# A two-block transformer on one Trainium2 core: the opening stage issued in one written order, with half of the first gate computed on TensorE

## The chip, the core and the metric

The kernel runs on one core of a Trainium2 chip. The core has five engines with a queue each: TensorE for matmuls (PE; its weight loads are shown as PEld), VectorE (DVE), ScalarE (ACT), GpSimd (POOL) and SyncE, whose queue (SP) issues nearly all loads from the chip's memory. Each engine works through its own queue in order; semaphores tie the queues together. The metric is the device time of one execution in microseconds, lower is better. Of the kernel before there are three timed runs, with a median of 959.78 us (957.72 to 960.89), and one profiled execution.

## The reference, cut to what matters

Two blocks run one after the other on a sequence of 256 tokens of width 1024. The first block is two layers deep: a causal pooling layer and an attention layer, each followed by an MLP with a squared ReLU (1024 to 4096 to 1024), and all of them modulated by rows that are computed from a condition vector `c`. The second block mixes a gated delta rule with a forgetting attention and ends in a SwiGLU. Nothing of the change lies behind the first MLP's first chunks, so this is the part that counts (layer 0):

```python
c_act = jax.nn.silu(c)
mod = c_act @ w_mod[0] + b_mod[0]                      # 1024 x 6144, read once
sh1, sc1, g1, sh2, sc2, g2 = jnp.split(mod, 6, axis=-1)
h = modulate(rmsnorm(x, norm_mix[0]), sh1, sc1)        # h * (1 + sc1) + sh1
y = pool_mixer(h, w_pool[0], pool_scale[0])            # trailing means, 4 groups of 256 channels
x = x + g1[:, None, :] * y
h = modulate(rmsnorm(x, norm_mlp[0]), sh2, sc2)
x = x + g2[:, None, :] * squared_relu_mlp(h, w_up[0], w_down[0])
...
def pool_mixer(h, w_pool, pool_scale):                 # per group g: (window mean - token) @ w_pool[g]
    ...
    return y * pool_scale
def squared_relu_mlp(h, w_up, w_down):
    a = jax.nn.relu(h @ w_up)
    return (a * a) @ w_down
```

All tensors are float32. Products of full precision are made of three matmuls on split operands: a high part (`_h`, `_hi`), which ACT rounds, and a low part (`_l`, `_lo`), the rest, which DVE subtracts.

## The kernel before, in words

The 256 tokens are two tiles of 128. Weights arrive in loads of 512 KB or 1 MB (128 partitions of 4 or 8 KB) and are split in pieces of 128x1024 by one ACT and one DVE instruction each (`piece_hi`, L275, and `piece_lo`, L281).

Everything from the first load to the first two of the eight chunks of the first MLP's up projection is one stage, in which all five queues follow the order in which the program issues (`manual_schedule`). The steps of this stage, with the names that the order lists and the prediction use:

- The rows `c` and the columns of biases and norms (`vecs`), `x` and the pooling bands are loaded. `crow` is silu(c) on all partitions, `c32` silu(c) as columns. The norm factors of `x` (`n0`) are worked out and `x` is multiplied by them (L759).
- Sections: a half (512 columns) of one of the six modulation parts comes as two loads of 1 MB (`wms`, SP L680), is multiplied by `c32` on PE (`sec`, L722: 4 matmuls of 32x512 for each load, which the trace counts as 8), copied by ACT (`secr`, L727), turned into a column of four blocks on PE (`secc`, L734) and finished by DVE (L741, L744). Before, the mixer's scale and shift and the MLP's scale are made in this way.
- Columns: the mixer's gate and the MLP's shift are made on DVE, by one multiply-and-sum of 128x1024 for each of the eight blocks of 128 channels (`wmp`, L807, and `wms`, L459), from loads of 512 KB per block.
- Pooling: window sums on PE (`pk`, L751 to L753), scale on ACT (L771), shift on DVE (L775), split (L779, L782), the products with `w_pool` (`pool`, L292 to L294), the gate on ACT (`pool_o`, L813), transposes to token rows (`xadd`, L820) and the additions to `x` (L526).
- The MLP's norm: sums of squares on ACT (L358), factors (L686, L341 to L352), the normalized tokens (`mlp_xn`, L839 on DVE and L841 on ACT), transposes to feature columns (`mlp_tp`, L848), scale and shift on ACT (`mlp_hf`, L856), split.
- The up projection of chunks 0 and 1: for each of eight blocks of channels and each of the two chunks 6 matmuls of 128x512 (`up<-wu_...,mlp_...`), 96 in all; the weights are `wu00` and `wu01`, two loads of 1 MB each, split in four pieces. Two loads of chunk 2 (`wu02`) close the stage.

Loads go into three pools of buffers: `mraw` (two of 1 MB), `raw` (three of 1 MB) and the pieces (five pairs `whi`, `wlo` of 512 KB each). SP waits for a buffer at the issue of its load, and what stands behind in its queue waits too. The loads' own semaphores let eight loads be under way.

The order of this stage is made by `Plan`: each step has an engine, a cost in us and its needs; the planner walks through time and takes what can start first, the longest remaining way first. Loads keep the order in which they are written down. Three lines show the kind:

```python
plan = Plan({"dma": 3.0, "vec": 11.0, "act": 9.5, "pe": 6.0})
op(f"win{g}", "pe", 2.6, [], windows, g)
op(n, "vec", 1.4, [f"g1{kt // 2}"], lambda kt=kt: gate_sum(kt, loaded[f"g1{kt // 2}"][kt % 2]))
```

Behind the stage the chunks follow one another (`up` of 128x256 for the next chunk, `dn` for the down projection), in an order that the scheduler sets.

Of the kernel before, what the change touches and what calls it, by code (L numbers as in the profile page):

```python
# [14 lines left out]
P = 128  # L15
# [124 lines left out]
class Plan:  # L140

    LAG = {"dma": 1.1}

    def __init__(self, free):
        self.free, self.ops = dict(free), {}

    def op(self, name, eng, cost, needs, f, *args):
        self.ops[name] = [eng, cost, list(needs), f, args]  # L150

    def run(self):
        ops = self.ops
        way = {}
        after = {n: [] for n in ops}
        for n, o in ops.items():
            for k in o[2]:
                after[k].append(n)

        def to_end(n):  # L160
            if n not in way:
                way[n] = ops[n][1] + max([to_end(k) for k in after[n]], default=0.0)
            return way[n]

        loads = [n for n, o in ops.items() if o[0] == "dma"]
        done, order, left = {}, [], dict(ops)
        while left:
            ready = []
            for n, (eng, cost, needs, _, _) in left.items():
                if eng == "dma" and n != loads[0] or any(k not in done for k in needs):  # L170
                    continue
                t = max([self.free[eng]] + [done[k] for k in needs])
                ready.append((t, -to_end(n), n))
            first = min(ready)
            eng, cost = ops[first[2]][:2]
            t, _, n = min((r for r in ready if ops[r[2]][0] == eng and r[0] <= first[0] + 0.02), key=lambda r: r[1])
            if eng == "dma":
                loads.pop(0)
            self.free[eng] = t + cost
            done[n] = t + cost + self.LAG.get(eng, 0.1)  # L180
            order.append((t, n))
            del left[n]
        self.done = done
        for t, n in order:
            ops[n][3](*ops[n][4])


def build(tc, a, out):
# [4 lines left out]
    with ctx:  # L193
# [139 lines left out]

        def rsqrt_col(v, n, name, rows=P, scale=1.0):

            y = work.tile([P, n], F32, tag=f"rs_y{n}", name=f"{name}_y", bufs=4)
            h = work.tile([P, n], F32, tag=f"rs_h{n}", name=f"{name}_h", bufs=2)
            t = work.tile([P, n], F32, tag=f"rs_t{n}", name=f"{name}_t", bufs=2)
            y, h, t = y[:rows], h[:rows], t[:rows]
            if n <= 2:  # L340
                pool.tensor_tensor(y, v, halves_of[:rows, :n], ALU.pow)  # L341
            else:
                vec.tensor_scalar(y.bitcast(I32), v.bitcast(I32), -0.5, RSQRT_MAGIC, ALU.mult, ALU.add)
            steps = 1 if n <= 2 else 3
            vec.tensor_scalar(h, v, -0.5 * (scale if steps == 1 else 1.0), None, ALU.mult)
            for i in range(steps):
                if n == 1:
                    vec.scalar_tensor_tensor(t, y, y, h, ALU.mult, ALU.mult)
                else:
                    vec.tensor_tensor(t, y, y, ALU.mult)  # L350
                    vec.tensor_tensor(t, t, h, ALU.mult)
                vec.scalar_tensor_tensor(y, t, 1.5 * (scale if steps == 1 else 1.0), y, ALU.add, ALU.mult)  # L352
            assert steps == 1 or scale == 1.0
            return y
# [347 lines left out]
        ones1 = [t2k(f"ones1{hf}") for hf in range(2)]
        for hf in range(2):
            ps = acc_tile(f"ones1p{hf}")
            pe.matmul(ps, ones[:1], rows0[:1, D + hf * 512:D + (hf + 1) * 512], start=True, stop=True)
            act.activation(ones1[hf], ps, AF.Copy)

        def section_load(sec, hf, q, where):  # L710
            src = a["w_mods"][sec, hf, q]
            return first_load(where, (src[:, :1024], src[:, 1024:]), f"wms{sec}{hf}{q}")

        sums32 = {}

        def section_product(sec, hf, q, rr):
            if q == 0:
                sums32[sec, hf] = acc_tile(f"sec{sec}{hf}")
            ps = sums32[sec, hf]
            for k in range(4):  # L720
                rows = slice(32 * k, 32 * k + 32)
                pe.matmul(ps[rows], c32[:, 4 * q + k], rr[k // 2][:, k % 2 * 512:(k % 2 + 1) * 512], start=q == 0,  # L722
                          stop=q == 1)

        def section_rows(sec, hf):
            t = t2k(f"secr{sec}{hf}")
            act.activation(t, sums32[sec, hf], AF.Copy)  # L727
            sums32[sec, hf] = t

        def section_turn(sec, hf):  # L730
            t = sums32[sec, hf]
            ps = sums32[sec, hf] = acc_tile(f"secc{sec}{hf}")
            for k in range(4):
                pe.matmul(ps[:, k:k + 1], t[:, k * P:(k + 1) * P], ones[:, 0:1], start=True, stop=True)  # L734

        def section_columns(sec, hf):
            s = (1, 0, 4)[sec]
# [16 lines left out]

        ss = [sums_of(x[:, t], f"n0{t}") for t in range(2)]
        y = pair_rstd(ss, "n0")
        xn0 = [big_tile(f"n0{t}")[:, :D] for t in range(2)]
        for t in range(2):
            vec.tensor_scalar(xn0[t], x[:, t], y[:, t:t + 1], None, ALU.mult)  # L759
        pks = [(mm_tile, tp_tile)[g % 2](f"pk{g}").rearrange("p (k n) -> p k n", k=2) for g in range(4)]  # L760
        def windows(g):
# [1366 lines left out]
```

## Time and profile before

| what | value |
|---|---|
| median of three timed runs | 959.78 us (957.72 to 960.89) |
| the profiled execution's own time | 960.81 us |
| its span, first to last instruction | 959.0 us |
| mean granted clock of TensorE | 0.98 |
| PE, PEld busy | 914.6 us (95%), 799.3 us (83%) |
| DVE, ACT busy | 642.4 us (67%), 497.7 us (52%) |
| loaded over the span | 198.31 MB, mean 207 GB/s |

The profiled execution takes 1.81 us more than its span and 1.03 us more than the median of the timed runs. All times below are us from the start of the span. In the 40 slices of the page (24 us each) PE is busy for 6, 7 and 6 tenths of the first three and for 9 from then on, but for two slices of 8 and the last of 6. The 96 matmuls of the first two up chunks begin at 68.53 and the next chunk's at 93.61: between these times and the start lies the stage that is changed.

### The profile page before, as it was taken

How to read it: one execution, taken by the hardware profiler on the slowest of the kernel's cores; microseconds unless marked ns; L12 is line 12 of the kernel's file. 1: busy time of each engine (PE TensorE's matmuls, PEld its weight loads, DVE VectorE, ACT ScalarE, POOL GpSimd, SP SyncE). 2: the span in 40 equal slices, each digit the busy share in tenths (PEclk: the TensorE clock that was granted, in tenths of full speed). 3: DMA queues.
4: the chain of work that ended last, by engine and by line, in shares of the span. 5: the costliest groups of instructions: out<-in, count | busy, mean ns of one | idle time of the engine just before them, and what ended most of it. 6: DMA issues, size and time to landing. Idle time of an engine off the chain costs nothing.

```text
span 959.0 us, 15265 instructions
## 1 busy us (share of the span) xinstructions
PE 914.6 (95%) x6021; PEld 799.3 (83%) x6021; DVE 642.4 (67%) x1230; ACT 497.7 (52%) x881; POOL 12.5 (1%) x22
## 2 busy tenths in 40 slices
PE   6769999999998999999999998999999999999996
PEld 3548889988797987889999967899988799999995
DVE  1587789789698674885556567698557765454544
ACT  2465535445466674644455535676455564444442
POOL 0000000000000000000000002000000000000000
PEclk9779999999999999999999999899999999999998
DMA  9979879889466460785565644233022555555531
GB/s 349 419 314 352 286 291 405 338 287 376 147 234 250 157 228 33 266 284 181 192 222 176 211 144 151 78 120 129 11 79 89 198 175 177 181 187 203 176 132 45
DMA packets 34555, 198.31 MB, mean 207 GB/s; under 512 B 4186, under 2 KB 6818, under 8 KB 14002
## 3 DMA queue, kind: packets, MB, share of 16 engines
q1 hardware_dynamic: 34484, 197.34, 57.8%
q8 instruction: 47, 0.77, 0.3%
q14 instruction: 24, 0.20, 0.1%
HBM read 196.24 MB, written 1.09 MB: 206 GB/s over the span
## 4 chain that ended last, share of the span: by engine, by line
PE 84%; DVE 5%; DMA 4%; issue 2%; ACT 2%; POOL 0%; SPq 0%; DVEq 0%; POOLq 0%; ACTq 0%
PE up L292 6%; PE up L293 6%; PE up L294 6%; PE dn L292 6%; PE dn L293 6%; PE dn L294 6%; PE gu L294 4%; PE gu L293 4%; PE gu L292 4%; PE qk L321 3%; PE fd L293 2%; PE fd L292 2%; PE fd L294 2%; DMA wms<-in_w_mods_dram 2%; PE cp L292 1%
## 5 line engine op out<-in xcount | busy, mean ns | idle before, releaser
L292 PE MATMUL up<-mlp_hi,wu_h 128*128 128x256 f32 x416 | 118.4, 285 | 0.0
L293 PE MATMUL up<-mlp_lo,wu_h 128*128 128x256 f32 x416 | 118.0, 284 | 0.0
L294 PE MATMUL up<-mlp_hi,wu_l 128*128 128x256 f32 x416 | 117.8, 283 | 0.0
L275 ACT ACTIVATE wd_h<-wd_r 128x1024 fp32r<-128x1024 f32 x58 | 61.4, 1059 | 74.1 <-PE up L293 44.1
L281 DVE TENSOR_TENSOR wd_l<-wd_r,wd_h 128x1024 fp32r<-128x1024 f32 x58 | 70.8, 1223 | 40.2 <-ACT wd_h L275 40.0
L275 ACT ACTIVATE wu_h<-wu_r 128x1024 fp32r<-128x1024 f32 x58 | 60.9, 1062 | 61.9 <-PE dn L294 47.0
L292 PE MATMUL dn<-wd_h,a 128*128 128x512 f32 x232 | 91.8, 396 | 0.0
L293 PE MATMUL dn<-wd_l,a 128*128 128x512 f32 x232 | 90.8, 392 | 0.0
L292 PE MATMUL gu<-f_hi,wgu_h 128*128 128x256 f32 x320 | 90.7, 283 | 0.0
L294 PE MATMUL gu<-f_hi,wgu_l 128*128 128x256 f32 x320 | 90.6, 283 | 0.0
L293 PE MATMUL gu<-f_lo,wgu_h 128*128 128x256 f32 x320 | 90.6, 283 | 0.0
L294 PE MATMUL dn<-wd_h,a 128*128 128x512 f32 x232 | 90.3, 389 | 0.0
L281 DVE TENSOR_TENSOR wu_l<-wu_r,wu_h 128x1024 fp32r<-128x1024 f32 x58 | 70.3, 1223 | 27.0 <-ACT wu_h L275 26.9
L281 DVE TENSOR_TENSOR wgu_l<-wgu_r,wgu_h 128x1024 fp32r<-128x1024 f32 x44 | 53.6, 1225 | 51.2 <-ACT wgu_h L275 51.2
L292 PEld LDWEIGHTS up<-mlp_hi,wu_h 128*128 128x128 f32 x416 | 79.7, 192 | 1.0 <-issue 0.5
L293 PEld LDWEIGHTS up<-mlp_lo,wu_h 128*128 128x128 f32 x416 | 79.7, 192 | 1.0 <-issue 0.5
L294 PEld LDWEIGHTS up<-mlp_hi,wu_l 128*128 128x128 f32 x416 | 79.8, 192 | 0.0
L275 ACT ACTIVATE wgu_h<-wgu_r 128x1024 fp32r<-128x1024 f32 x44 | 46.6, 1062 | 61.9 <-PE gu L293 29.4
L293 PEld LDWEIGHTS gu<-f_lo,wgu_h 128*128 128x128 f32 x320 | 61.4, 192 | 0.3
L292 PEld LDWEIGHTS gu<-f_hi,wgu_h 128*128 128x128 f32 x320 | 61.4, 192 | 0.4
L294 PEld LDWEIGHTS gu<-f_hi,wgu_l 128*128 128x128 f32 x320 | 61.4, 192 | 0.0
L292 PEld LDWEIGHTS dn<-wd_h,a 128*128 128x128 f32 x232 | 43.6, 188 | 10.0 <-issue 1.4
(770 smaller groups left out, 2286.3 us busy)
## 6 DMA issues: line engine op xcount, KB each, us to landing
wu_r<-in_w_up_dram SPq DMA_DIRECT2D x32, 1024.0 KB, 5.1
wd_r<-in_w_down_dram SPq DMA_DIRECT2D x32, 1024.0 KB, 5.3
wgu_r<-in_w_gu_dram SPq DMA_DIRECT2D x22, 1024.0 KB, 5.2
wmc<-in_w_modc_dram SPq DMA_DIRECT2D x16, 1024.0 KB, 7.1
wmg<-in_w_modg_dram SPq DMA_DIRECT2D x12, 1024.0 KB, 6.7
wfd_r<-in_w_fd_dram SPq DMA_DIRECT2D x11, 1024.0 KB, 4.9
wi_r<-in_w_in_dram SPq DMA_DIRECT2D x10, 1024.0 KB, 5.3
wqk_r<-in_w_qk_dram SPq DMA_DIRECT2D x8, 1024.0 KB, 5.8
```

Of the source, the lines that this page charges most:

```text
L275: act.activation(hi, r, AF.Copy)
L281: vec.tensor_tensor(lo, r, hi.bitcast(F32), ALU.subtract)
L292: pe.matmul(ps, l[0], r[0], start=first, stop=False)
L293: pe.matmul(ps, l[0], r[1], start=False, stop=False)
L294: pe.matmul(ps, l[1], r[0], start=False, stop=last)
L321: f(*a, **k)
```

## The change

`Plan` and its costs go; the steps are registered by name, and a written list, `FIRST_STEPS`, calls them in its order. A word of the list can carry the buffer pool of a load (`raw`, `mraw`, `split`) or the bank pool of a PE result (`acc`, `mm`, `tp`), which were fixed by rule before. Besides:

- `rows` (c) and `vecs` are loaded through ACT's queue; SP's first load is `x`.
- The squares of `x` are issued ahead of silu(c) on ACT, and the norm factors multiply the pooling bands (128x576 and 128x512 on DVE) where they multiplied `x` (two of 128x1024).
- The gate's second half (channel blocks 4 to 7) is made as a section (`s21`): two loads, two PE products, a copy, a turn and two small DVE operations, where it was four DVE sums. The first half stays on DVE. The loads have the same bytes.
- A section's turned column goes into the bank of its sums.
- One of the four sums of squares of the MLP's norm (tile 1, second half) is made on DVE. The norm factors are two steps (`y1`, `y2`), and another step can stand between them.

```diff
-class Plan:
-    ...
+FIRST_STEPS = """
+s101:mraw s001:mraw bn win2:acc s100:raw s000:raw wp:raw wph1 g2:split s00m0:acc ident s110:split s00m1
...
+        sq00 tok6 wu00 tok7 s30m0:acc add01 s30m1 add11 sq11 sq10 sq01 y1 col0 y2 s30r xn0v s30t ...
...
-        sp.dma_start(rows0[:1, :2 * D], a["c"])
+        act.dma_start(rows0[:1, :2 * D], a["c"])
...
-        sp.dma_start(vecs, a["vecs"])
+        act.dma_start(vecs, a["vecs"])
...
+        ss = [sums_of(x[:, t], f"n0{t}") for t in range(2)]
+        y0 = rsqrt_col(pair_sums(ss, "n0"), 2, "n0", scale=32.0)
         for hf, c in enumerate(halves):
             act.activation(crow[:, c], crp[hf], AF.Silu)
...
+        SECTIONS = (1, 0, 2, 4)
+        HALVES = ((0, 0), (0, 1), (1, 0), (1, 1), (2, 1), (3, 0), (3, 1))
...
         def section_turn(sec, hf):
-            t = sums32[sec, hf]
-            ps = sums32[sec, hf] = acc_tile(f"secc{sec}{hf}")
             for k in range(4):
-                pe.matmul(ps[:, k:k + 1], t[:, k * P:(k + 1) * P], ones[:, 0:1], start=True, stop=True)
+                pe.matmul(sums32[sec, hf][:, k:k + 1], secr[sec, hf][:, k * P:(k + 1) * P], ones[:, 0:1], start=True,
+                          stop=True)
...
+            if s == 2:
+                vec.tensor_tensor(gate[:, h4], col, vcol(V_BG)[:, h4], ALU.add)
+                vec.tensor_tensor(gate[:, h4], gate[:, h4], vcol(V_POOL)[:, h4], ALU.mult)
+                return
...
-        for t in range(2):
-            vec.tensor_scalar(xn0[t], x[:, t], y[:, t:t + 1], None, ALU.mult)
...
+        def bands_normed():
+            vec.tensor_scalar(bands[:, B_FIRST:], bands[:, B_FIRST:], y0[:, 0:1], None, ALU.mult)
+            vec.tensor_scalar(bands[:, :B_FIRST], bands[:, :B_FIRST], y0[:, 1:2], None, ALU.mult)
...
+            sq = t2k("poolsq")
+            vec.tensor_tensor_reduce(out=sq, in0=xs, in1=xs, scale=1.0, scalar=0.0, op0=ALU.mult, op1=ALU.add,
+                                     accum_out=ss[t][:, hf:hf + 1])
...
-        def norm_factors():
-            ys.append(pair_rstd(ss, "mlp0n"))
+        def norm_factors(first):
+            if first:
+                ys.append(pair_sums(ss, "mlp0n"))
+                ys.append(rsqrt_guess(ys[0], 2, "mlp0n", scale=32.0))
+            else:
+                ys[0] = rsqrt_step(*ys[1], 2, 32.0)
...
-        plan.run()
+        for word in FIRST_STEPS.split():
+            name, *where = word.split(":")
+            f, args = steps.pop(name)
+            f(*args, *where)
...
-    d["w_mods"] = f(wm[0, [1, 0, 4]])
+    d["w_mods"] = f(np.concatenate([wm[0, 1], wm[0, 0], wm[0, 2, 1:], wm[0, 4]]))
...
-    d["w_modp"] = f(wc[0, [2, 3]])
+    d["w_modp"] = f(np.concatenate([wc[0, 2, :4], wc[0, 3]]))
```

Names in the order below: `wmsAB...` are loads of section A (before: 0 scale, 1 shift, 2 MLP scale; now 2 is the gate and 3 the MLP scale), half B; `wmp0`, `wmp1` (before `wmp` and `wms0` to `wms6`) loads of the gate's and the MLP shift's columns.

SP's queue around the loads of the up weights, before:

```order
L680 DMA wms211_432<-in_w_mods_dram 128x1024 x2
L220 DMA wu00_r0_450<-in_w_up00_dram 128x2048
L220 DMA wu01_r0_462<-in_w_up00_dram 128x2048
L680 DMA wms0_480<-in_w_modp_dram 128x1024 x2
L680 DMA wms2_506<-in_w_modp_dram 128x1024 x2
L220 DMA wu00_r2048_526<-in_w_up00_dram 128x2048
L220 DMA wu01_r2048_572<-in_w_up00_dram 128x2048
L680 DMA wms4_594<-in_w_modp_dram 128x1024 x2
L680 DMA wms6_622<-in_w_modp_dram 128x1024 x2
```

and now:

```order
L190 DMA wu01_r0_307<-in_w_up00_dram 128x2048
L698 DMA wms300hi_315<-in_w_mods_dram 128x1024
L698 DMA wms300lo_316<-in_w_mods_dram 128x1024
L698 DMA wms301hi_387<-in_w_mods_dram 128x1024
L698 DMA wms301lo_388<-in_w_mods_dram 128x1024
L738 DMA wmp10_440<-in_w_modp_dram 128x1024 x2
L698 DMA wms310_463<-in_w_mods_dram 128x1024 x2
L190 DMA wu00_r0_471<-in_w_up00_dram 128x2048
L698 DMA wms311hi_512<-in_w_mods_dram 128x1024
L698 DMA wms311lo_513<-in_w_mods_dram 128x1024
L738 DMA wmp12_549<-in_w_modp_dram 128x1024 x2
L738 DMA wmp14hi_592<-in_w_modp_dram 128x1024
```

Before, all four loads of `wu00` and `wu01` and both of the MLP scale's second half stood ahead of the last four shift columns, with `wu01_r2048` waiting for a `raw` buffer in the midst. Now `wu01_r0` stands ahead of the MLP scale, and the loads alternate between sections, columns and up weights.

DVE's queue from the additions to `x` on, before:

```order
L526 TENSOR_TENSOR x_81<-xadd00_411,x_81 128x512
L526 TENSOR_TENSOR x_81<-xadd10_412,x_81 128x512
L281 TENSOR_TENSOR wu00_l0_488<-wu00_r0_450,wu00_h0_487 128x1024
L526 TENSOR_TENSOR x_81<-xadd01_483,x_81 128x512
L526 TENSOR_TENSOR x_81<-xadd11_484,x_81 128x512
L459 ISA wms0_480,modcol0_102<-wms0_480,crow_96,vecs_84 128x1024
L459 ISA modcol0_102 128x1
L741 TENSOR_TENSOR modcol0_102<-secc20_490,vecs_84 128x4
L744 SCALAR_TENSOR_TENSOR modcol0_102<-modcol0_102,vecs_84 128x4
L686 TENSOR_SCALAR mlp0n_v_530<-pool0_ss_154 128x1
L686 TENSOR_SCALAR mlp0n_v_530<-pool1_ss_155 128x1
L345 TENSOR_SCALAR mlp0n_h_534<-mlp0n_v_530 128x2
```

and now:

```order
L251 TENSOR_TENSOR wu01_p0_423<-wu01_r0_307,wu01_p0_423 128x1024
L507 TENSOR_TENSOR x_81<-xadd00_395,x_81 128x512
L507 TENSOR_TENSOR x_81<-xadd10_396,x_81 128x512
L507 TENSOR_TENSOR x_81<-xadd01_452,x_81 128x512
L507 TENSOR_TENSOR x_81<-xadd11_453,x_81 128x512
L828 ISA poolsq_486,pool1_ss_147<-x_81 128x512
L828 ISA pool1_ss_147 128x1
L663 TENSOR_SCALAR mlp0n_v_492<-pool0_ss_146 128x1
L663 TENSOR_SCALAR mlp0n_v_492<-pool1_ss_147 128x1
L310 TENSOR_SCALAR mlp0n_h_496<-mlp0n_v_492 128x2
L440 ISA wmp10_440,modcol0_102<-wmp10_440,crow_96,vecs_84 128x1024
L440 ISA modcol0_102 128x1
```

Before, a weight piece (`wu00_l0`) stood between the two pairs of additions, and a column sum with two small operations between them and the norm's sums. Now the four additions and a sum of squares follow each other, and the column sum stands inside the norm factors, behind `mlp0n_h`.

PE's queue from the transposes of the normalized tokens to the first up matmuls, before:

```order
L848 MATMUL mlp0_tp2_575<-ident_85,mlp0_xn0_542 128x128
L848 MATMUL mlp0_tp2_575<-ident_85,mlp0_xn1_544 128x128
L292 MATMUL up000_584<-wu00_h0_487,mlp0_hi_156 128x512
L293 MATMUL up000_584<-wu00_l0_488,mlp0_hi_156 128x512
L294 MATMUL up000_584<-wu00_h0_487,mlp0_lo_157 128x512
L292 MATMUL up001_588<-wu00_h0_487,mlp0_hi_156 128x512
L293 MATMUL up001_588<-wu00_l0_488,mlp0_hi_156 128x512
L294 MATMUL up001_588<-wu00_h0_487,mlp0_lo_157 128x512
```

and now:

```order
L854 MATMUL mlp0_tp1_528<-ident_85,mlp0_xn0_506 128x128
L854 MATMUL mlp0_tp1_528<-ident_85,mlp0_xn1_518 128x128
L706 MATMUL sec31_538<-wms310_463,c32_98 32x512 x4
L262 MATMUL up010_553<-wu01_p0_423,mlp0_hi_148 128x512
L263 MATMUL up010_553<-wu01_p0_423,mlp0_hi_148 128x512
L264 MATMUL up010_553<-wu01_p0_423,mlp0_lo_149 128x512
L262 MATMUL up011_557<-wu01_p0_423,mlp0_hi_148 128x512
L263 MATMUL up011_557<-wu01_p0_423,mlp0_hi_148 128x512
L264 MATMUL up011_557<-wu01_p0_423,mlp0_lo_149 128x512
```

Before, six blocks were transposed and the sections were all done when the up matmuls began, with chunk 0 ahead. Now the first product of the MLP scale's second half stands between four transposed blocks and the up matmuls, with chunk 1 ahead.

## Rows read from the trace of the kernel before

**Rows 1.** The page, the span in 40 slices: DMA engines' busy share, tenths

```profile
DMA  9979879889466460785565644233022555555531
```

**Rows 2.** Busy time of each engine, granted clock, DMA share, GB/s by 5 us

```profile
40.00:45.00 5.00, 4.00 (x17) 3.71 (x18) 4.96 (x17) 4.75 (x14) 0.00 (x0) 0.50 1.03 422
...
60.00:65.00 5.00, 0.84 (x5) 0.79 (x5) 3.92 (x13) 3.88 (x8) 0.70 (x1) 0.50 0.71 297
65.00:70.00 5.00, 4.30 (x16) 3.46 (x17) 5.00 (x9) 4.50 (x8) 0.00 (x0) 0.50 0.28 61
```

**Rows 3.** The chain that ended last: start, length, what (0 to 140 us)

```profile
21.21 11.68 DMA wpool<-in_w_pool_dram
...
68.17 0.31 ACT mlp_hi L779
...
68.53 0.80 PE up L292
```

**Rows 4.** What SP's queue waited for, total, times, longest (0 to 110 us)

```profile
SPq L220 <- DVE wu_l L281: 28.6, 4, 11.3
```

**Rows 5.** SP's issues in order of time: start, length, what

```profile
0.73 0.35 SPq L299 DMA_DIRECT2D rows<-in_c_dram  x1
...
1.55 0.89 SPq L304 DMA_DIRECT2D x<-in_x_dram  x2
...
67.58 0.33 SPq L220 DMA_DIRECT2D wu_r<-in_w_up_dram  x1
```

**Rows 6.** The first two up chunks by granted clock, busy as in Rows 2

```profile
68.53:73.59 5.06, 5.06 (x12) 3.96 (x13) 4.91 (x11) 2.03 (x4) 0.00 (x0) 0.50 0.96 343
73.59:84.64 11.05, 11.05 (x51) 9.05 (x49) 9.33 (x14) 3.94 (x8) 0.00 (x0) 1.00 0.82 296
```

**Rows 7.** PE in order of time: section product, turn, transposes, chunk 2's first matmul

```profile
51.07 1.07 PE L722 MATMUL sec<-wms,c 128*32 128x512 f32 x8
...
55.07 0.95 PE L734 MATMUL secc<-ones,secr 128*128 128x1 f32 x8
...
64.92 2.91 PE L848 MATMUL mlp_tp<-ident,mlp_xn 128*128 128x128 f32 x12 [4.16 <-DVE mlp_xn L839]
...
93.61 0.28 PE L292 MATMUL up<-mlp_hi,wu_h 128*128 128x256 f32 x1
```

**Rows 8.** ACT splits that waited for a load, in order of time

```profile
57.78 1.06 ACT L275 ACTIVATE wu_p<-wu_r 128x1024 fp32r<-128x1024 f32 x1 [0.50 <-DMA wu_r<-in_w_up_dram]
...
72.80 1.06 ACT L275 ACTIVATE wu_p<-wu_r 128x1024 fp32r<-128x1024 f32 x1 [2.97 <-DMA wu_r<-in_w_up_dram]
```

**Rows 9.** Groups by line, 0 to 95 us: busy, mean ns, idle before

```profile
L807 DVE CUSTOM_DVE_ANT_0 wmp<-wmp,crow,vecs 128x1024 f32<-128x1024 f32 x8 | 10.2, 1278 | 0.0
L281 DVE TENSOR_TENSOR wu_l<-wu_r,wu_h 128x1024 fp32r<-128x1024 f32 x8 | 9.5, 1220 | 2.4 <-ACT wu_h L275 2.4
L275 ACT ACTIVATE wu_h<-wu_r 128x1024 fp32r<-128x1024 f32 x8 | 8.0, 1048 | 0.7 <-DMA wu_r<-in_w_up_dram 0.7
...
L813 ACT ACTIVATE pool_o<-pool,gate 128x256 f32<-128x256 f32 x8 | 3.6, 473 | 5.8 <-DVE gate L809 3.1 <-DVE pool_lo L782 2.7
L727 ACT ACTIVATE secr<-sec 128x512 f32<-128x512 f32 x6 | 3.5, 591 | 13.2 <-PE sec L722 13.2
L782 DVE TENSOR_TENSOR mlp_lo<-mlp_hf,mlp_hi 128x256 fp32r<-128x256 f32 x8 | 3.2, 420 | 4.8 <-ACT mlp_hi L779 4.8
L526 DVE TENSOR_TENSOR x<-xadd,x 128x512 f32<-128x512 f32 x4 | 2.6, 681 | 0.0
L839 DVE TENSOR_SCALAR mlp_xn<-x,mlp0n_y 128x512 f32<-128x512 f32 x2 | 0.9, 481 | 0.0
```

**Rows 10.** The pool products' tile alone, busy by stretch, as in Rows 2

```profile
47.57:50.75 3.18, 3.18 (x24) 2.99 (x24) 1.31 (x3) 1.00 1.04 425
```

**Rows 11.** DVE in order of time: the MLP norm's factors, first and last

```profile
61.66 0.21 DVE L686 TENSOR_SCALAR mlp0n_v<-pool_ss 128x1 f32<-128x1 f32 x1 [0.34 <-ACT pool_sq L358]
...
63.08 0.16 DVE L352 SCALAR_TENSOR_TENSOR mlp0n_y<-mlp0n_t,mlp0n_y 128x2 f32<-128x2 f32 x1
```

More of the change, by code (lines that the diff above doesn't have):

```diff
@@ L137, in costing @@
         yield cost
-class Plan:
[L144 to L185, printed above, removed]
@@ new lines @@
+s301:split s21t tok0:mm:tp po3 po2 prod2:mm gate1 plo7 s21c po1 wuh10 tok1 prod3:acc sh0:raw tok2 tok3 po4 sh1
+wul10 po5 tok4:tp:acc po6 tok5 add00 po7 s310:mraw add10 sq00 tok6 wu00 tok7 s30m0:acc add01 s30m1 add11 sq11
+sq10 sq01 y1 col0 y2 s30r xn0v s30t s311:split wuh11 xn1v feat0:acc xn0a s30c feat1 feat2:mm feat3 col1 xn1a
+mhf0 mhi0 s31m0:mm mhf1 mhi1 wuh00 sh2:mraw sh3 mlo0 up10 feat4:tp mlo1 wul11 up11 wul00 wuh01 s31m1 up00 feat5
+wul01 col2 sh4:split s31r col3 mhf2 mhi2 s31t mlo2 s31c up01 mhf3 mhi3 up12 wu11 col4 mhf4 mlo3 mhi4 mlo4
@@ L188, in build @@
+feat6:tp sh5 up02 wu01 wuh12 wuh13 sh6:split col5 mhf5 wul12 feat7 mhi5 wul13 wuh02 mlo5 sh7 wul02 wuh03 up13
+col6 up03 up14 mhf6 up15 col7 mhi6 mlo6 wul03 up04 mhf7 up05 wu21 up16 up06 mhi7 mlo7 up07 up17 wu20
+"""
 def build(tc, a, out):
@@ L332, in build, with rsqrt_guess @@
         pool.memset(halves_of, -0.5)
+        def rsqrt_guess(v, n, name, rows=P, scale=1.0):
+            y = work.tile([P, n], F32, tag=f"rs_y{n}", name=f"{name}_y", bufs=4)[:rows]
+            h = work.tile([P, n], F32, tag=f"rs_h{n}", name=f"{name}_h", bufs=2)[:rows]
+            t = work.tile([P, n], F32, tag=f"rs_t{n}", name=f"{name}_t", bufs=2)[:rows]
+            pool.tensor_tensor(y, v, halves_of[:rows, :n], ALU.pow)
+            vec.tensor_scalar(h, v, -0.5 * scale, None, ALU.mult)
+            return y, h, t
@@ L346, in rsqrt_col @@
[L346 to L353, printed above, removed]
+                return rsqrt_step(*rsqrt_guess(v, n, name, rows, scale), n, scale)
@@ new lines, in rsqrt_col @@
+            assert scale == 1.0
+            y = work.tile([P, n], F32, tag=f"rs_y{n}", name=f"{name}_y", bufs=4)[:rows]
+            h = work.tile([P, n], F32, tag=f"rs_h{n}", name=f"{name}_h", bufs=2)[:rows]
+            t = work.tile([P, n], F32, tag=f"rs_t{n}", name=f"{name}_t", bufs=2)[:rows]
+            vec.tensor_scalar(y.bitcast(I32), v.bitcast(I32), -0.5, RSQRT_MAGIC, ALU.mult, ALU.add)
+            vec.tensor_scalar(h, v, -0.5, None, ALU.mult)
+            for _ in range(3):
+                y = rsqrt_step(y, h, t, n)
@@ L703, in build @@
         for hf in range(2):
[L704 to L716 removed]
+            act.activation(ones1[hf], ones1p[hf], AF.Copy)
@@ new lines, in build, with step @@
+        steps = {}
+        loaded = {}
+        banks = {"acc": acc_tile, "mm": mm_tile, "tp": tp_tile}
+        def step(name, f, *args):
+            steps[name] = f, args
+        SECTIONS = (1, 0, 2, 4)
+        HALVES = ((0, 0), (0, 1), (1, 0), (1, 1), (2, 1), (3, 0), (3, 1))
+        sums32 = {}
+        secr = {}
+        def section_load(sec, hf, q, where):
+            src = a["w_mods"][HALVES.index((sec, hf)), q]
+            r = loaded[sec, hf, q] = first_tile(where, f"wms{sec}{hf}{q}")
+            for k in range(2):
+                sp.dma_start(r[k], src[:, k * 1024:(k + 1) * 1024])
@@ new lines, in build @@
+        step("ident", lambda: sp.dma_start(ident, a["ident"]))
+        step("wp", load_pool)
+        for sec, hf in HALVES:
+            n = f"s{sec}{hf}"
+            for q in range(2):
+                step(f"{n}{q}", section_load, sec, hf, q)
+                step(f"{n}m{q}", section_product, sec, hf, q)
+            step(n + "r", section_rows, sec, hf)
+            step(n + "t", section_turn, sec, hf)
+            step(n + "c", section_columns, sec, hf)
+        for g in range(4):
+            step(f"win{g}", windows, g)
+            step(f"prod{g}", pool_product, g)
```

217 lines of the change are left out of this document (87 added, 130 removed).

## The prediction

> **What bounds the kernel now.** First the page's slices: the DMA engines are 9 tenths busy in slices 1 and 2, 7 in the third, 9 in the fourth [rows 1]. The windows of 5 us show the hole inside: 0.71 of the DMA share from 60 to 65 and 0.28 from 65 to 70, at 61 GB/s, where 422 GB/s flow in 40 to 45 [rows 2]. The chain of waits, read next, is a load up to about 33, and then small steps up to the first up matmul at 68.53 [rows 3]. SP's own waits name the hole: the longest is 11.3 us for `wu_l` on DVE [rows 4], the wait before the up load that is issued at 67.58 [rows 5]. So the stage is limited by loads first, then by a chain of short steps (pool products, additions, norm, transposes), and from 68.53 by PE: 12 matmuls in 5.06 us at a granted clock of 0.50 (1.2 GHz), the others 0.23 apart at 1.00 (2.4 GHz): 48 begin in the 11.05 us of the second window, whose count of 51 takes in some that only reach into it [rows 6]. At 93.61 chunk 2 takes over [rows 7]; from there on the page's slices of PE hold 9 tenths, as told above. What the change is worth is therefore how much earlier the 96 up matmuls end.
>
> **Loads.** A MiB takes 2.49 us: the split that waited for its load until 57.78 stands 10.0 MiB behind `wpool`, which landed at 21.21 + 11.68 = 32.89 as the 10.67th MiB [rows 3, 8]. SP issued `rows` at 0.73 and `x` at 1.55 [rows 5]; with two loads on ACT's queue `x` goes 0.82 earlier, and I move all landings by that. Landing of MiB c is then 32.07 + 2.49 (c - 10.67). In the new order: `s111`, last of the mixer's scale and shift, c = 11.67, at 34.6; `s211`, last of the gate's section, 14.17, at 40.8; `g1` 42.0; `wu10` 44.5; `s301` 49.5; `sh0` 50.7; `wu00` 57.0; `wu11` 65.7; `wu01` 69.4; `sh7` 71.9. A buffer wait delays nothing if it ends before the load's turn would come anyway, some 10 us ahead of its landing (`wpool` took 11.68 [rows 3]). By the chain below all do but two: `wu11` waits for the column sum `col1` (some 57) and `wu01` for the split `wul11` (some 60). At those times the loads ahead of them (to `sh4` at 63.2, to `sh5` at 66.9) are still under way, so the engines have work, and I cost both waits at nothing; if that cover is gone, see D.
>
> **The chain up to the norm.** `s111` at 34.6, its product 1.07, copy 0.59, two turns of 0.95 on PE [rows 7, 9]: 37.6. Two pool products of 12 matmuls each, 24 in 3.18 at full clock [rows 10]: 40.8. Two gate products, 2 x 1.07: 42.9; copy 43.5; turn 44.5; two small DVE operations behind a column sum of 1.28 and a low part of 0.42 whose load landed at 42.0 [rows 9]: 45.4. This replaces four DVE sums, 4 x 1.28 = 5.1, which were on DVE when it was full. Two more pool products with four transposes between, from 44.5: 49.1 on PE (a transpose is 2.91/12 = 0.24 at the lower clock, half at the upper) [rows 7]; two `pool_o` of 0.47 behind the last, one more pair of transposes: 49.8. Two additions of 0.68 [rows 9], back to back (no weight piece between them now): 51.1. The last sum of squares on DVE, half of a 128x1024 sum, 0.64, an estimate: 51.8. The norm's factors took 63.24 - 61.66 = 1.58 before [rows 11]; a column sum of 1.28 now stands inside, of which the GpSimd step hides about 0.7: 54.0. Before: 63.24.
>
> **Up to the first up matmul.** Two normalizations of 0.48: 54.9. Eight transposes at 0.24, since I expect PE at 0.50 here as before: 56.8. Section product of `s310` ahead of the up matmuls, at the lower clock, at most twice 1.07: 58.9. Meanwhile ACT and DVE have the operands ready (scale and high part 0.47 each, low part 0.42). First up matmul 58.9, before 68.53.
>
> **The up matmuls.** 5.06 for the first 12, 84 x 0.23 = 19.3 [rows 6], eight transposes beside them at 0.12, one section product of 1.07, one turn of 0.95: 27.4, so 86.3. DVE must keep up: from the first low part on 8 x 0.42 + 7 weight pieces x 1.22 + 6 column sums x 1.36 (with the small instruction behind each) = 20.1, and two groups of 6 matmuls behind its last: no later than about 83. PE is the later of the two. 93.61 - 86.3 = 7.3 gained.
>
> The rows on the clock: it was 0.50 in 40 to 45 and 60 to 70, after PE had stood idle, and rose 5.06 us after the up matmuls began [rows 2, 6]. The Trainium skill (TensorE: Matmul & The Clock Gate, section "HAM oscillation — how this bites in real kernels") says that groups of matmuls with waits between them can start at the lower clock every time. By it, up matmuls that are fed piece by piece might never rise; the time by it is rival E.
>
> **What is given back.** My chain has no handovers; one in the trace is 0.05 (`mlp_hi` ends at 68.48, PE starts at 68.53) [rows 3], others under 0.2, over some 15 steps 1.2, an estimate (0.5 to 3). Behind the up matmuls ACT's queue now has `up000r` ahead of the four splits of chunk 2, where the splits stood ahead: `up000r` can start 2 us before the end, so the first low part comes 0.59 + 1.05 + 1.22 later, 0.8 behind the end, where chunk 2's third matmul wants it: 0.5, between 0 and 1.5. Sum: 7.3 - 1.2 - 0.5 = 5.6.
>
> **Costed at nothing.** The second ACT table load, which the squares ahead of silu(c) bring, and the bands' scaling (two of 0.48, like a normalization [rows 9]) end by about 13.5, and only window products wait for them; PE's sections are paced by landings until 34.6, so even 4 us more there stay hidden behind the loads. Were that cover gone, the price would be those us one for one. The norm factors on the bands leave the number of PE's window matmuls as it was. The free banks add no wait: each bank's last reader is done when its next product comes.
>
> The profiled execution took 960.81, its span 959.0. 960.81 - 5.6 = 955.2; the median of the runs shown is 1.03 lower, so I predict 959.78 - 5.6 = 954.2. From no change a measurement of this kernel can tell 0.3%, 2.9 us: faster is below 956.9, slower above 962.7.
>
> **Rivals.**
> B, the lower clock in the pool products too. For it: it was 0.50 in 40 to 45, when they started before [rows 2]; against it: then PE had run out of work ahead of them, and now it has sections up to 37.6. Price: half of 5.06, less what the wait for `s211` hides, 2.3, 956.5.
> C, no lower clock at all from the pool products on, since the holes are shorter. The transposes cost 1.0 less, the section product 1.0, the up matmuls 5.06 - 12 x 0.23 = 2.3: PE ends at 82.0, and DVE is nearly the bound. 4.3 more: 949.9. Against it: between the last section turn (some 53.5) and the transposes at 54.9 PE has nothing to do.
> D, the loads are the limit after all. `wu01` issued into an empty queue lands 5.2 us later (67.58 to 72.80) [rows 5, 8], its splits take 2.3, and six groups of 6 matmuls, 8.2, are behind it. No gain is left if it is issued at 93.1 - 15.7 = 77.4, against 60 in my chain. For it: SP's order has thirteen loads behind buffers; against it: the 17 us. 959.5.
> E, slower. PE gets its operands piece by piece and stays at 0.50 through the stage. Price: 96 x 5.06/12 = 40.5, with transposes, product and turn 45.6 from 58.9: 104.5, 10.9 later than before, with the 1.7 given back 972.4. It decides once the lower clock lasts past about 75: each us beyond 64 costs half a us, and 5.6 are to be lost. Against it: at the lower clock PE is slower than DVE, so operands pile up and no wait is left to keep it low; before, the clock rose although DVE was 4.91 of 5.06 busy [rows 6].
>
> **Chances.** Forecast 0.45 (952 to 957), B 0.20, C 0.19, D 0.09, E 0.07. Faster: the forecast, C and six in ten of B, 0.76; within 0.3%: the rest of B and D, 0.17; slower: E, 0.07. The range goes from C to just under D, 949.5 to 959.0; it takes in the handovers' 0.5 to 3 and the 0 to 1.5 behind the stage, and leaves out E, most of D and the edge of C.
>
> **What would show it.** DMA share near 1.0 from 10 to 70 without the hole; the longest wait of SP's queue under 5 us; the norm's last DVE step near 54; first up matmul near 59; a granted clock of 0.50 for about 5 us from there; 128x512 matmuls ending near 86 to 88; chunk 2's first low part the only wait behind them. Wrong: a hole ahead of `wu11` or `wu01`, PE waiting for `mlp_lo` or `wu_l` within the up matmuls, or a stage that ends early while chunk 2 or the first `dn` matmuls behind it wait.

## The result, and the profile after

The changed kernel takes 947.57 us (median of 4 runs, 945.92 to 952.14), the kernel before beside it 959.88: a ratio of 0.9875, 95% interval 0.9856 to 0.9894. The forecast was 954.2, in 949.5 to 959.0. The direction and the place were right; the gain is 12.3 us where 5.6 were forecast, and the time lies below the range. The profiled execution took 948.82 with a span of 947.0 (before 960.81 and 959.0), so the two traces have 12.0 us between them.

The page's slices answer to [rows 1]: the DMA engines are at 8 or 9 tenths in all of the first four.

```profile
PEclk9999999999998999999999999999999999999998
DMA  9998899989194560875565643242112555555541
```

The windows of 5 us, with columns as in [rows 2], show the hole gone: 424 and 422 GB/s in 60 to 65 and 65 to 70, where 297 and 61 flowed. The granted clock is 1.00 in 40 to 45, where it was 0.50, and of the first 120 us only two windows lie below 1.00.

```profile
40.00:45.00 5.00, 4.28 (x38) 2.72 (x37) 3.80 (x11) 4.25 (x10) 0.00 (x0) 1.00 0.99 413
50.00:55.00 5.00, 3.14 (x23) 2.25 (x16) 4.83 (x15) 3.51 (x7) 0.70 (x1) 0.86 1.02 424
55.00:60.00 5.00, 5.00 (x24) 2.69 (x24) 3.95 (x7) 3.66 (x6) 0.00 (x0) 0.80 1.03 420
60.00:65.00 5.00, 5.00 (x32) 3.32 (x31) 4.37 (x9) 2.46 (x5) 0.00 (x0) 1.00 1.02 424
65.00:70.00 5.00, 5.00 (x25) 4.07 (x24) 4.20 (x8) 4.15 (x7) 0.00 (x0) 1.00 1.02 422
```

SP's waits from 55 to 95 (total, times, longest): the stage's longest, 5.6, stands ahead of chunk 2's second load, issued at 70.77; the 7.8 lies behind the stage, ahead of a load of the down weights, issued at 84.39.

```profile
SPq L190 <- DVE wu_l L251: 13.3, 3, 7.8
SPq L190 <- DVE mlp_lo L778: 5.6, 1, 5.6
```

VectorE in order of time: the norm's factors begin at 50.61 and are done at 52.73 + 0.16 = 52.89, where [rows 11] end at 63.24.

```profile
50.61 0.33 DVE L663 TENSOR_SCALAR mlp0n_v<-pool_ss 128x1 f32<-128x1 f32 x2
...
52.73 0.16 DVE L320 SCALAR_TENSOR_TENSOR mlp0n_y<-mlp0n_t,mlp0n_y 128x2 f32<-128x2 f32 x1
```

TensorE in order of time (answers to [rows 3, 7]): transposes, the section product of `s310`, the first up matmul at 57.24, chunk 2 at 82.26, its third matmul with the one wait, and the first `dn` matmul.

```profile
53.46 2.15 PE L854 MATMUL mlp_tp<-ident,mlp_xn 128*128 128x128 f32 x8 [1.12 <-DVE mlp_xn L846]
55.55 1.76 PE L706 MATMUL sec<-wms,c 128*32 128x512 f32 x8
57.24 0.50 PE L262 MATMUL up<-wu_p,mlp_hi 128*128 128x512 f32 x1
...
82.26 0.28 PE L262 MATMUL up<-mlp_hi,wu_h 128*128 128x256 f32 x1
82.38 0.28 PE L263 MATMUL up<-mlp_lo,wu_h 128*128 128x256 f32 x1
83.28 0.38 PE L264 MATMUL up<-mlp_hi,wu_l 128*128 128x256 f32 x1 [0.62 <-DVE wu_l L251]
...
96.36 0.40 PE L262 MATMUL dn<-wd_h,a 128*128 128x512 f32 x1
```

The first `dn` matmul of the kernel before:

```profile
106.85 0.40 PE L292 MATMUL dn<-wd_h,a 128*128 128x512 f32 x1
```

So the stage gives 106.85 - 96.36 = 10.49. Stretches by granted clock, answers to [rows 6]: the lower level (1.2 GHz) lies over the transposes and the section product; the 96 up matmuls run at 2.4 GHz from the first on.

```profile
53.50:57.00 3.50, 3.50 (x16) 1.66 (x16) 2.42 (x7) 2.81 (x7) 0.00 (x0) 0.51 1.00 417
57.00:82.26 25.26, 25.26 (x124) 19.81 (x121) 18.27 (x29) 13.73 (x22) 0.00 (x0) 1.00 1.02 418
```

The other 1.5 us appear 450 us later, ahead of the first `fv` matmul behind the second MLP. Before, ScalarE stood there 5.46 us for a small load, with half of a normalization behind it:

```profile
572.72 0.20 ACT L1463 ACTIVATE ea<-grow 128x4 f32<-128x4 f32 x1 [5.46 <-DMA grow<-in_gate_consts_dram]
572.83 0.70 ACT L578 ACTIVATE u_xn<-u_q,uy 128x512 f32<-128x512 f32 x1
```

SP had issued that load behind a wait of its own for VectorE:

```profile
SPq L1392 <- DVE beta L1453: 12.4, 1, 12.4
```

In the changed kernel, whose code there is the same but whose scheduler starts from other times, the load is issued 11.6 us behind the first matmul of the last `dn` block (547.44) instead of 23.8 (568.70), and ScalarE's step is over before the normalization:

```profile
558.13 0.19 ACT L1430 ACTIVATE ea<-grow 128x4 f32<-128x4 f32 x1
562.31 0.72 ACT L559 ACTIVATE u_xn<-u_q,uy 128x512 f32<-128x512 f32 x1 [3.99 <-DVE uy L554]
```

From the last block of `dn` matmuls to the first `fv` matmul it is 577.39 - 544.89 = 32.50 before and 566.89 - 535.85 = 31.04 after. All profiles below agree: 32.50 to 32.55 in the four with this wait (before, a4, b3, c3), 31.04 to 31.05 in the eleven without it.

Two more differences between these two profiles cancel. In attention the changed kernel's has 6.8 us at the lower clock (from 285.70) where the other has 3.4 (from 298.85), and its lead shrinks from 10.5 to 9.05 at the first `wo` matmul (353.04 and 343.99). Behind the first `fv` matmul it is the other way, 3.4 (from 596.31) against 6.8 (from 606.06), and the lead grows from 10.50 to 12.03 at the first `g0ktp` matmul (625.89 and 613.86). Such stretches differ between executions of one program: in a1, the changed kernel again, they were 3.4 and 6.8.

### The profile page after: what moved, and what is told of

Its sections match the earlier page's. It is cut to its first block, busy times and chain, and to the rows that moved or that the text cites. A ratio compares the mean times of both kernels' runs of the same rounds, so it can differ in the third digit from the quotient of the medians.

```text
span 947.0 us, 15295 instructions
## 1 busy us (share of the span) xinstructions
PE 913.9 (97%) x6045; PEld 795.4 (84%) x6045; DVE 638.7 (67%) x1222; ACT 498.2 (53%) x881; POOL 12.5 (1%) x22
## 4 chain that ended last, share of the span: by engine, by line
PE 84%; DVE 6%; DMA 4%; issue 3%; ACT 3%; POOL 0%; SPq 0%; DVEq 0%; POOLq 0%; ACTq 0%
PE up L262 6%; PE up L264 6%; PE up L263 6%; PE dn L264 6%; PE dn L263 6%; PE dn L262 6%; PE gu L263 4%; PE gu L264 4%; PE gu L262 4%; PE qk L291 2%; DMA wms<-in_w_mods_dram 2%; PE fd L262 2%; PE fd L263 2%; PE fd L264 2%; PE cp L262 1%
## 5 line engine op out<-in xcount | busy, mean ns | idle before, releaser
L251 DVE TENSOR_TENSOR wgu_l<-wgu_r,wgu_h 128x1024 fp32r<-128x1024 f32 x44 | 53.6, 1225 | 51.3 <-ACT wgu_h L245 51.3
```

The costliest lines, as they stand in the source:

```text
L251: vec.tensor_tensor(lo, r, hi.bitcast(F32), ALU.subtract)
```

## The experiments

Two theories. **K**: the forecast charged the lower clock to the wrong work, and the stage is now bound by TensorE, so that each us at the lower clock costs half a us. **S**: the steps are shorter than summed, and the clock has no part. The marks of each profile, in us (lower: how long the granted clock was 0.50 between 50 and chunk 2; before it is 59.9 to 73.6, in b1 two stretches of 3.4, the first ahead of its norm):

| run | norm done | first up | chunk 2 | first dn | lower |
|---|---|---|---|---|---|
| before | 63.24 | 68.53 | 93.61 | 106.85 | 13.7 |
| after | 52.89 | 57.24 | 82.26 | 96.36 | 3.4 |
| a1, as after | 53.31 | 57.83 | 83.86 | 97.96 | 6.8 |
| c1, as after | 53.04 | 55.92 | 81.08 | 95.19 | none |
| a2 splits first | 52.83 | 57.35 | 83.40 | 96.19 | 6.8 |
| a3 clock kept | 53.29 | 56.18 | 81.22 | 95.33 | none |
| b4 both | 52.92 | 55.81 | 80.94 | 93.73 | none |
| c2 both | 52.70 | 55.58 | 80.71 | 93.50 | none |
| b1 gate on VectorE | 56.28 | 60.59 | 85.62 | 98.41 | 6.8 |
| b2 x normed | 52.98 | 57.50 | 83.50 | 97.60 | 6.8 |
| c4 product behind | 52.78 | 55.41 | 83.12 | 97.21 | 3.4 |
| a4 before, filled | 65.68 | 70.21 | 95.29 | 108.53 | 3.4 |
| b3 before, filled | 63.01 | 68.30 | 92.64 | 105.88 | none |
| c3 before, gate | 68.96 | 73.70 | 96.84 | 110.07 | 13.7 |
| d1 before, ea | 63.32 | 68.60 | 93.89 | 107.13 | 13.7 |

**a1 and c1, the changed kernel again.** 

> The changed kernel once more, as the base of this group. Two theories for why it gained 12.3 us where 5.6 were forecast. Theory K (clock): the sum charged the lower TensorE clock to the wrong work; it held 0.50 from 53.6 to 57.0 only, over the transposes and a section product, and not over the first 12 up matmuls (5.06 us forecast, 2.8 measured); 10.5 us are gained in the stage, and the rest, 1.5, is two lower stretches of the clock further on that happened to be 6.8 us then 3.4 in this execution against 3.4 then 6.8 before. Theory S (steps): the steps up to the first up matmul are simply shorter than summed, and the clock has no part in it. K expects single runs of this kernel to lie up to some 6 us apart, each us of a run going with 2 us at the lower clock (mean granted clock 0.987 at the long end, 0.994 at the short). S expects no such link. Both: 945 to 952, median near 947.6.

> The changed kernel once more, as the base of this group: 945.4 to 952.2, median 946 to 948, shorter runs with a higher mean clock.

Measured: medians 946.69 (6 runs, 0.9875, 0.9851 to 0.9898) and 947.94 (4 runs, 0.9861, 0.9846 to 0.9876). Of the 14 runs, the four with a mean clock of 0.994 took 945.41 to 945.92, the two with 0.987 took 951.87 and 952.14. A clock lower by 0.007 over 947 us is 13.3 us more at the lower level, for 6.4 us more time: about half, as K says (the mean clock is given to 0.001, or 1.9 us, and the four runs at 0.993 lie between 946.05 and 948.77). The same program had 3.4, 6.8 and no us of it in the same place. In a1's profile it reaches 2 us into the up matmuls. K's other part, that two later stretches of the clock make the last 1.5 us, is out: they cancel, as told above.

```profile
53.05:59.88 6.83, 5.99 (x21) 3.40 (x22) 5.68 (x13) 5.08 (x8) 0.00 (x0) 0.50 1.01 415
```

**a2, splits first.** Two steps behind the stage's last, and a fence ahead of the first relu:

```diff
+w2h0 w2l0 w2h1 w2l1                       (end of FIRST_STEPS)
...
+            step(f"w2h{h}", wu02.piece_hi, h)
+            step(f"w2l{h}", wu02.piece_lo, h)
...
-act.activation(r, src, AF.Relu)
+with later() if name == "up000" else ExitStack():
+    act.activation(r, src, AF.Relu)
```

> The changed kernel, with the first two weight splits of chunk 2 ahead of the first relu on ScalarE's queue and their low parts behind the last low part of the stage on VectorE's. In the changed kernel chunk 2's third matmul waits 0.62 us for the first low part. If that wait is what the order on ScalarE costs: no wait there, 0.6 to 0.8 us less than the changed kernel of this group. If the load of that weight is the limit: the splits wait for it and the time is the same within 0.3.

Measured: the wait is gone, and from chunk 2 to the first `dn` it is 12.79 us instead of 14.10, so the order on ScalarE cost 1.3, not the 0.6 to 0.8 expected. The median, 948.43 (6 runs, 944.55 to 950.23; 0.9875, 0.9851 to 0.9899), doesn't show it: the runs' clocks lay between 0.988 and 0.995. By the profile only.

**a3, clock kept.** Transposes of the identity into a bank that is free, 6 ahead of `s30t` and 9 behind it:

```diff
-... s30r xn0v s30t s311:split ...
+... s30r xn0v fillA s30t fillB s311:split ...
...
+pe.transpose(pouts[2][:, 0, :P], ident, ident)     (x6, x9)
```

> The changed kernel, with 15 transposes of the identity into a free bank that nobody reads: 6 ahead of the column turn at 51.3 us and 9 behind it, where TensorE stands for 0.74 and 1.12 us. Theory K: the granted clock stays 1.00 through 50 to 60; the eight transposes take 1.2 instead of 2.15 and the product 1.05 instead of 1.69, so the first up matmul begins at 55.6 to 55.9 instead of 57.24, chunk 2 near 80.7 instead of 82.26, and the time is 1.3 to 1.6 us less. Theory S: the first up matmul is held by the operands, not by TensorE: no change, within 0.4.

Measured: 946.51 (4 runs, 945.02 to 946.97; 0.9859, 0.9840 to 0.9878), which doesn't show the 1.3 to 1.6 against a1's 946.69. Windows, transposes, product and first up matmul of its profile:

```profile
50.00:55.00 5.00, 4.86 (x43) 3.42 (x35) 4.79 (x16) 3.84 (x8) 0.70 (x1) 1.00 1.03 424
...
55.00:60.00 5.00, 5.00 (x33) 2.69 (x31) 4.30 (x7) 3.72 (x6) 0.00 (x0) 1.00 1.02 417
```

```profile
53.87 1.38 PE L854 MATMUL mlp_tp<-ident,mlp_xn 128*128 128x128 f32 x8
55.18 1.07 PE L706 MATMUL sec<-wms,c 128*32 128x512 f32 x8
56.18 0.50 PE L262 MATMUL up<-wu_p,mlp_hi 128*128 128x512 f32 x1
```

From the norm to chunk 2 it takes 27.93, against 29.37 in the changed kernel's first profile and 30.55 in a1: K holds: 3.4 us at the lower clock cost 1.4 here, 6.8 cost 2.6 (a2 and b2, with 6.8 too, take 30.57 and 30.52). But c1, without the extra transposes, had 28.04 by itself; what they seem to buy is that it is so each time: no lower stretch in the three profiles with them (a3, b4, c2), one without it among the six that lack them and keep the gate's section (after, a1, c1, a2, b2, c4).

**a4 and b3, the kernel before with TensorE filled.** 17 such transposes ahead of the last column turn and 28 behind it:

```diff
+if (sec, hf) == (2, 1): fill(17)     (ahead of the turn)
+if (sec, hf) == (2, 1): fill(28)     (behind it)
+pe.transpose(xadd[0, 0][:, P:2 * P], ident, ident)   (a4: sums32[2, 0])
```

> The kernel before, with 45 transposes of the identity that nobody reads: 17 ahead of the last column turn at 59.38 us and 28 behind it, so that TensorE doesn't stand ahead of the norm's transposes. Theory K: the clock stays 1.00, the transposes take 1.7 instead of 2.9 and the first 12 up matmuls 2.8 instead of 5.06: up to 3.2 us less than the kernel before, less what VectorE (4.91 of 5.06 us busy there) then holds back, so 1 to 3.2 less. Theory S: the clock costs nothing that VectorE would not cost: the same within 0.5.

> The kernel before with the same 45 transposes of the identity as in the run a4, now into a bank that the additions have already read: in a4 they wrote the bank of a column turn whose reader on VectorE stood behind them, so VectorE waited 2.9 us for them and the norm came 2.4 us later; the first dn matmul, though, only 1.7. Theory K: without that wait the clock is 1.00 from the transposes on, and the first dn matmul comes 0.8 to 3 us earlier than 106.85. Theory S: VectorE, 4.9 of 5 us busy from 65 on, holds the up matmuls at either clock: within 0.5 of 106.85.

Measured: a4 963.19 (8 runs; 1.0033, 1.0021 to 1.0046), longer, as neither theory had it, by a flaw of the edit: VectorE stood 2.9 us for the bank. b3 960.55 (12 runs; 0.9999, 0.9988 to 1.0009): the clock is at its upper level through the stage, the up matmuls start 0.23 apart, and the first `dn` is only 0.97 earlier. TensorE now waits there, for ScalarE and VectorE:

```profile
68.30 0.50 PE L292 MATMUL up<-wu_h,mlp_hi 128*128 128x512 f32 x1 [1.89 <-ACT mlp_hi L787]
...
71.96 0.50 PE L292 MATMUL up<-wu_p,mlp_hi 128*128 128x512 f32 x1 [1.21 <-DVE modcol L749]
```

By the forecasts 0.97 is the low end of K (0.8 to 3) and outside S (within 0.5). But it is one seventh of the 6.9 that half of 13.7 would give, and the median shows none of it: in the kernel before, TensorE at the upper clock waits for ScalarE and VectorE instead. In the changed kernel K holds. Why the median shows nothing of the 0.97 stays open.

**b1 and c3, the gate's half, undone and alone.**

```diff
 b1: -s210:split ... s211:mraw ... s21m0:acc s21m1 s21r s21t s21c
     +g4:split g5 ... g6:mraw g7 ... gate4 gate5 gate6 gate7
 c3: +section(3, (None, None, "raw", "raw"), (1,))   (in the old planner, for gate4 to gate7)
```

> The changed kernel, with the gate's second half back on VectorE: the two section loads, four products' worth of matmuls, copy, turn and columns become four column loads of the same bytes in the same places and four sums of 1.28 us with a small instruction each (5.7 us on VectorE), between the last low part of the pooling and the split's low part. If VectorE is the path to the norm there (it has some 2 us of idle time between 43 and 47.5): the additions start 2 to 4 us later, and the kernel is 2 to 4 us longer than the changed one. If VectorE's idle time and TensorE's freed time hide it: within 0.5. Times are compared with half of the time at the lower clock taken out, since that differs from run to run (939.8 for the changed kernel so, 0.4 either way).

> The kernel before with one part of the change alone: the second half of the pooling's gate as a section on TensorE, ordered by the old planner. In the old order VectorE is 4.9 of 5 us busy from 35 to 55, and the part takes 5.1 us of sums out of it. If VectorE is the path to the norm in the old order too: the norm's last step 3 to 5 us earlier than 63.24 and the kernel 2 to 4.5 us shorter than before (956 to 958.5). If the searched order is what makes the part pay (the section's wait for its load, copy and turn late in the old order): within 1 of before.

Measured: b1 950.10 (5 runs, 948.93 to 950.75; 0.9891, 0.9876 to 0.9906); the norm is done 3.0 to 3.4 later than in the changed kernel's profiles, and the median 2.9 us above the 947.2 of that kernel's 14 runs. At chunk 2 b1 is 3.4 behind the changed kernel's first profile; from there to the first `dn` it takes 12.79 against 14.10, since here the scheduler put the four splits ahead of the first relu on ScalarE (80.67 and 84.48), the order that a2 made by hand. So the part is worth some 3.4 us in the stage, of which b1 gets 1.3 back by another way. The other 7 us by which the norm comes earlier than before (the order, the loads on ACT's queue, the sum of squares on VectorE) weren't taken apart. c3 goes the other way: 965.32 (5 runs; 1.0041, 1.0027 to 1.0054), the norm 5.7 later. Among its waits, ScalarE has two weight splits, which wait for their load, ahead of the gated products:

```profile
55.21 2.00 ACT L275 ACTIVATE wu_h<-wu_r 128x1024 fp32r<-128x1024 f32 x2 [2.01 <-DMA wu_r<-in_w_up_dram]
57.12 0.46 ACT L818 ACTIVATE pool_o<-pool,gate 128x256 f32<-128x256 f32 x1
```

The part takes 5.1 us from VectorE in both orders, and pays only in the one made with it. How much each of c3's waits costs wasn't taken apart.

**b2, norm factors on x.** `vec.tensor_scalar(xn0[t], x[:, t], y0[:, t:t + 1], ...)` in place of the two on the bands.

> The changed kernel, with the mixer's norm factors put on x again (two of 128x1024 on VectorE into a tile of their own) in place of on the bands (two of some 0.5 us), ahead of the window products. The forecast costed this part at nothing, since the window products wait for nothing but it and TensorE's sections are paced by loads until 34: within 0.4 of the changed kernel with half of the lower clock's time taken out. If the early part is on the path after all: up to 1.2 us longer.

Measured: 948.59 (6 runs, 945.00 to 950.89; 0.9876, 0.9856 to 0.9895), chunk 2 at 83.50 against a1's 83.86 with the same lower stretch: no effect, as forecast.

**c4, product behind.** `s31m0:mm` from ahead of `mhf1` to behind `up10`.

> The changed kernel with the section product of the second half's first load behind the first two groups of up matmuls instead of ahead of them. The forecast had the product on the path to the first up matmul (2.1 us at the lower clock) and again 5.06 us for the first 12 up matmuls behind it. Theory K: TensorE does the same work in another order and the lower stretch is as long; first up matmul about 1 us earlier, chunk 2 within 0.5 of the changed kernel's 81.2 to 83.9, according to the length of the lower stretch; same median within 1. By the forecast's own reckoning: the 12 take 5.06 at the lower clock from the first on, the stage is 1 to 2 us shorter.

Measured: 950.14 (4 runs, 948.78 to 950.89; 0.9887, 0.9873 to 0.9900). The first up matmul is 1.8 earlier and chunk 2 is 0.9 later than in the changed kernel's profile. The lower stretch is 3.41 us in both; here TensorE stands 0.67 us for the first high part, which the product had covered. K's mark for chunk 2 held, its median didn't (the four runs have mean clocks of 0.988 to 0.992); the forecast's reckoning, a shorter stage, is out.

```profile
55.41 0.78 PE L262 MATMUL up<-wu_p,mlp_hi 128*128 128x512 f32 x1 [0.67 <-ACT mlp_hi L775]
```

**b4 and c2, both edits, the better version.**

> The changed kernel with both edits that looked useful alone: the first two splits of chunk 2 ahead of the first relu on ScalarE (a2: 1.27 us earlier behind the stage than a1 in profiles with the same 6.8 us at the lower clock), and the 15 transposes that keep the clock at 1.00 ahead of the norm's transposes (a3: no lower stretch in the stage). Expected: no lower stretch before 90 us, no wait of chunk 2's third matmul, the first dn matmul at 94.5 (96.36 in the changed kernel's profile, 95.33 in a3), and a median of 945.0 to 946.0.

> The kernel of b4 once more, to have it beside the changed kernel on the same chip: no lower stretch in the stage, median 944.8 to 945.8, 1 to 2.5 less than c1, and runs that lie closer together.

Measured: 945.11 (5 runs, 943.69 to 947.67; 0.9851, 0.9832 to 0.9869) and 945.63 (5 runs, 944.78 to 946.82; 0.9841, 0.9828 to 0.9855). Over all runs 945.4 (10) against 947.2 for the changed kernel (14); the intervals of the ratios overlap, so the 1.8 is likely, not shown by the times. The profile shows its place: the first `dn` at 93.73 and 93.50.

**d1, the kernel before without the wait ahead of the normalization.**

```diff
-act.activation(ea, grow[:, 12:16], AF.Exp)
+with tc.issue_after(last_on(mybir.EngineType.Activation)):
+    act.activation(ea, grow[:, 12:16], AF.Exp)
```

> The kernel before with one instruction moved: ScalarE's exponential of the decay row (128x4), which waited 5.5 us for its load ahead of the normalization's second half at 572, goes behind the other exponentials near 600. If that wait is what the changed kernel has lost there: from the first of the 96 dn matmuls to the first fv matmul 31.0 instead of 32.5 us, the kernel 1.3 to 1.5 us shorter than before (ratio 0.9985). If not: 32.5 as before and no change.

Measured: 957.14 (10 runs, 956.33 to 959.51) against 960.75 beside it, 0.9968 (0.9957 to 0.9979). From the last `dn` block to the first `fv` matmul 576.32 - 545.27 = 31.05, as in the changed kernel: the cause of the 1.46 is settled. The time gained more than that; in the profiles the rest is the clock's. From 590 to 620, where the kernel before has a mean clock of 0.89, this profile has 1.00. From the first `fv` to the first `g0ktp` matmul the profiles of either kernel take 45.4 where no lower stretch lies between (d1, a3, b1, b4, c4), 47.0 with 3.4 us of it (after, a2, c1, c2, b3) and 48.5 to 48.6 with 6.8 (before, a1, b2, c3): here TensorE is waited for, and the price is about half in both kernels. d1's 45.36 against 48.50 is the other 3.1 us of its profile's lead. Whether the edit makes that stretch rarer wasn't tested; four runs of the kernel before as it is, with mean clocks of 0.984 to 0.986, took 956.86 to 957.52, as long as d1's median, so the times alone don't show the edit's worth.

```profile
590.00:620.00 30.00, 28.64 (x218) 25.59 (x218) 21.34 (x52) 18.90 (x36) 0.98 (x1) 1.00 0.48 165
```

## Why the prediction was wrong, point by point

**The step that failed** is the lower clock in the terms from the norm to chunk 2: "5.06 for the first 12", the transposes at 0.24 and the product at twice 1.07. I let the lower level start anew with the up matmuls, because in [rows 6] it ended 5.06 us behind their start. In the changed kernel TensorE works without a hole from the first transpose on, and the level was back at 57.0, before the first up matmul. I charged 4.3 us in all, and 1.4 were paid in this execution: norm to chunk 2 took 29.37 against 28.0 without any lower stretch (c1 28.04, a3 27.93), and I had 32.3. Without the 4.3 my sum is 28.0, so the count of work was right. How much is paid is luck of the execution: in a1 the level was back only at 59.88, and 2.5 of the 4.3 were paid; three of the 14 runs (950.06, 951.87, 952.14) lie inside the range. Over the gap between 949.9 and 954.2 I chose the forecast over rival C; C had this part right. The reason given against C, that TensorE has nothing to do ahead of the transposes, is true and does bring the clock down (53.6), but not for as long as I thought.

**The chain up to the norm** was 54.0, and with the 1.2 for handovers 55.2; measured 52.89, 2.3 less. Loads and pool products came 0.4 to 0.7 early (`s111` at 34.2, the second product done at 40.1). The additions, of which I had left only two for the end, are four in a row of 2.48 us, but begin at 47.5, not 49.8. Without the 1.2 the sum is 54.0, and the chain ended 1.1 ahead even of that, so no handovers of this size show: the first sum of the norm begins 0.03 behind the additions, the normalization 0.03 behind the factors.

**ScalarE's order behind the stage** cost 0.86 against the kernel before (chunk 2 to `dn` 14.10 against 13.24), where I had 0.5.

Together 5.6 + 2.3 + 2.9 - 0.36 = 10.4 of the stage's 10.49: both theories have a part, the clock 2.9 and shorter steps 2.3. The second step that failed is the sentence that the gain is what the up matmuls end earlier: it takes the rest of the program as fixed, and the scheduler that orders it gave 1.46 more (d1). 10.5 + 1.5 is the 12.0 between the spans, the two later stretches of the clock cancelling.

**What held.** The hole in the loads is gone and the loads weren't the limit, and the pool products ran at the upper clock, so D and B are out: the up load that D needed by 77.4 was issued at 58.4. The bands, the banks and the second table load cost nothing that shows (b2 undid the bands; the free banks and the table load weren't undone alone). VectorE doesn't bind from the norm on: its last low part of the stage is done at 76.5, and a filled TensorE (b4) still reaches chunk 2 at 80.9. E's waits between the groups of up matmuls didn't come, and the clock rose.

**The price of the clock.** In the changed kernel 13.3 us more at the lower level went with 6.4 us more time; the kernel before, without its 13.7 us around the norm, gained 0.97 in the stage (b3, of it 0.74 behind the norm), since TensorE waited for others during them. The Trainium skill (TensorE: Matmul & The Clock Gate, section "HAM oscillation — how this bites in real kernels") counts half of such a stretch as its price. The changed kernel's runs agree; for the opening stage of the kernel before the measurement decides, and it was one seventh of that.

## What to carry to other kernels

A lower clock cost near half of its time where TensorE was the engine that was waited for, and a seventh of that half where it wasn't; before pricing it, ask what would be late next if it were gone, and count it as one stretch, not anew for each group of matmuls. Of an order that has been searched as a whole, a part taken alone can lose (c3) what it gains inside (b1). Where a scheduler orders the rest of the program, compare its queues there too: a small load behind a wait and an instruction in front of a critical one were worth 1.5 us, 450 us away from the change.

## What the runs showed of the hardware

The same program, run again, has the lower clock in one place for 3.4, 6.8 or no us, and its time goes with it: 945.4 to 952.1. Differences below some 3 us between two such kernels need profiles or many runs. 15 transposes that nobody reads, 2.1 us of them in TensorE's holes, went with a level of 2.4 GHz through the stage in all three profiles that had them; of the six without them one had it.
